# A SwiGLU stream whose tiles take every second half-MiB: from one contiguous block per tile to two interleaved tiles in 16 MiB

## The chip, the cores and the metric

The kernel runs on one NeuronCore of a Trainium2 chip. The metric is device time in microseconds of one execution, as the median of several runs. Beside it there is one profiled execution, whose trace gives every engine instruction and every DMA packet; its "span" runs from the first to the last event that the profile shows on the core.

## The reference

The input `x` is a float32 matrix of 8192 rows by 8192 columns (268.4 MB). Each row is split into a left half `a` and a right half `b` of 4096 columns, and the output is `a * b / (1 + exp(-b))`, a float32 matrix of 8192 by 4096 (134.2 MB):

```python
a, b = np.split(x, 2, axis=-1)
silu_b = b / (1 + np.exp(-b))
return a * silu_b
```

Nothing is reused: every input byte is read once and every output byte is written once, and rows are independent of each other. Which rows are put together in a tile is therefore free.

## The kernel before

A tile holds 256 rows: 128 partitions with `R = 2` consecutive rows each. In DRAM these two rows are 64 KiB of contiguous input, so a tile is a block of 128 x 64 KiB = 8 MiB of input and 128 x 32 KiB = 4 MiB of output. `xv` and `ov` (L30, L31) are the views that say so: row `p` of tile `i` in the view is row `i * 128 + p` of a matrix with 4096 rows of 64 KiB (`xv`) or 32 KiB (`ov`). There are 32 tiles, and three buffers of 64 KiB per partition in SBUF.

`load(i)` (L38 to L44) issues one DMA on SyncE's queue (SP) that brings the whole tile. The last tile is loaded in two halves, one row per partition each. `swiglu(i, k)` (L46 to L54) takes row `k` of each partition: ScalarE (ACT) computes SiLU of the right half in place (L49), and VectorE (DVE) multiplies it with the left half and puts the product where the output is collected, at the front of the same buffer (L50). `store(i)` (L56 to L59) issues one DMA of the 4 MiB product on ACT's queue; the last two tiles use SP's queue instead.

The order of the work is that of the program text, since the schedule is manual (L63). Three loads are issued up front (L67). Then for each tile come two `swiglu` calls, a store, and the load of the tile three further on (L75 to L80), which goes into the buffer that the store has just emptied. That load waits on SP until the store has landed. One small DMA stands ahead of everything: `zt`, 128 partitions of 128 zeros, is written to the front of each output row of tile 0 (L65) and is overwritten later by the first store.

What the change touches is the two views and their three uses, at L43, L58 and L65. The prediction also speaks of the rows that one DMA is made of: a load has 128 pieces of 64 KiB, one per partition, and a store 128 pieces of 32 KiB.

Of the kernel before, what the change touches and what calls it, by code (L numbers as in the profile page):

```python
# [1 line left out]

# [4 lines left out]

_SILU = mybir.ActivationFunctionType.Silu


@with_exitstack
def kernel(
    ctx: ExitStack,
    tc: tile.TileContext,
    x: bass.AP,
    out: bass.AP,
):

    nc = tc.nc
    N, M = x.shape
    half = M // 2
    P = nc.NUM_PARTITIONS
    R = 2
    BUFS = 3

    xv = x.tensor.reshape([N // R, R * M]).ap()  # L30
    ov = out.tensor.reshape([N // R, R * half]).ap()  # L31
    ntiles = N // (P * R)
    last = ntiles - 1

    pool = ctx.enter_context(tc.tile_pool(name="sbuf", bufs=BUFS))
    tiles = {}

    def load(i, rows=None):  # L38
        if i not in tiles:
            tiles[i] = pool.tile([P, R * M], x.dtype, name="xt")  # L40
        lo, hi = (0, R) if rows is None else rows
        nc.sync.dma_start(  # L42
            out=tiles[i][:, lo * M : hi * M], in_=xv[i * P : (i + 1) * P, lo * M : hi * M]  # L43
        )  # L44

    def swiglu(i, k, c0=0, cw=half):  # L46
        xt = tiles[i]
        b = xt[:, k * M + half + c0 : k * M + half + c0 + cw]
        nc.scalar.activation(out=b, in_=b, func=_SILU)  # L49
        nc.vector.tensor_mul(  # L50
            out=xt[:, k * half + c0 : k * half + c0 + cw],
            in0=xt[:, k * M + c0 : k * M + c0 + cw],
            in1=b,
        )  # L54

    def store(i, c0=0, cw=R * half):  # L56
        (nc.scalar if i < last - 1 else nc.sync).dma_start(
            out=ov[i * P : (i + 1) * P, c0 : c0 + cw], in_=tiles[i][:, c0 : c0 + cw]  # L58
        )  # L59


    zt = ctx.enter_context(tc.tile_pool(name="zeros", bufs=1)).tile([P, 128], x.dtype, name="zt")
    ctx.enter_context(tc.manual_schedule())  # L63
    nc.vector.memset(zt, 0.0)  # L64
    nc.scalar.dma_start(out=ov[0:P, 0:128], in_=zt)  # L65

    for i in range(BUFS):  # L67
        load(i)
    for i in range(last):
        for k in range(R):  # L70
            swiglu(i, k)
        if i == last - 1:
            swiglu(last, 0)
        store(i)
        nxt = i + BUFS  # L75
        if nxt < last:
            load(nxt)
        elif nxt == last:
            load(last, (0, 1))
            load(last, (1, 2))  # L80

    store(last, 0, half)
    for c0 in range(0, half, half // 2):
        swiglu(last, 1, c0, half // 2)
    store(last, half, half)


# [1 line left out]
_INS = ['x']  # L89
_OUTS = [((8192, 4096), 'float32')]  # L90


# [23 lines left out]
```

## Time and profile before

| | before |
|---|---|
| median of 3 runs | 936.15 us (936.01 to 936.37) |
| profiled execution, its own time | 935.73 us |
| its span | 933.9 us |
| DVE busy | 283.5 us (30%) |
| ACT busy | 229.4 us (25%) |
| bytes moved by DMA | 402.74 MB, mean 431 GB/s |
| median from issue to landing, 8 MiB load | 34.2 us |
| median from issue to landing, 4 MiB store on ACT's queue | 40.0 us |

The page of the profile gives, per engine, the busy time and its share of the span; for the DMA engines, the busy share in 40 equal slices and the rate in GB/s; for each DMA queue, the packets, the bytes, and the time that its packets took as a share of the time of 16 DMA engines; and the chain of work that ended last. Queue q1 carries SP's transfers (all loads, and the stores of the last two tiles), q10 carries ACT's (all other stores). Times in the views are microseconds from the start of the span.

### The profile page before, as it was taken

The page shows a single profiled execution, that of the slowest core. Times are in us where ns is not written, and L with a number is a line of the kernel's source. Part 1 is how long each engine was busy: PE and PEld are TensorE (multiplying, and loading weights), DVE is VectorE, ACT ScalarE, POOL GpSimd, SP SyncE. Part 2 cuts the span into 40 slices and gives each one's busy share as a digit, 9 for nine tenths or more (in the row PEclk, how much of TensorE's full clock was granted, in tenths as well). Part 3 has the DMA queues.
Part 4 walks back from the last instruction along what each step waited for, and adds up shares of the span by engine and source line. Part 5 has one row for each costly group of instructions (what it writes and reads, how often), then busy time and mean ns, then how long its engine had stood idle before and what let it go on. Part 6 is the DMA issues. An engine that isn't in the chain of part 4 may idle for free.

```text
span 933.9 us, 370 instructions
## 1 busy us (share of the span) xinstructions
DVE 283.5 (30%) x66; ACT 229.4 (25%) x66; POOL 0.2 (0%) x4
## 2 busy tenths in 40 slices
DVE  0333312333113332133321333213332133331252
ACT  0323330233312333113331133311333203332041
POOL 0000000000000000000000000000000000000000
DMA  9999999999999999999999999999999999999998
GB/s 407 422 413 460 411 431 441 449 427 420 456 408 445 431 431 441 435 422 441 448 414 436 435 451 425 429 443 414 446 427 436 436 432 425 439 451 411 441 434 383
DMA packets 9650, 402.74 MB, mean 431 GB/s; under 512 B 1072, under 2 KB 1200, under 8 KB 1200
## 3 DMA queue, kind: packets, MB, share of 16 engines
q1 hardware_dynamic: 5184, 276.83, 68.6%
q10 hardware_dynamic: 4464, 125.90, 31.2%
q14 instruction: 2, 0.02, 0.0%
HBM read 268.44 MB, written 134.28 MB: 431 GB/s over the span
## 4 chain that ended last, share of the span: by engine, by line
DMA 84%; DVE 10%; ACT 4%; DVEq 0%; issue 0%; SPq 0%; ACTq 0%
DMA out_dram<-xt 43%; DMA xt<-in_x_dram 41%; DVE xt L50 10%; ACT xt L49 4%; DVEq L111 0%; SPq L42 0%; ACTq L49 0%; DVEq L50 0%
## 5 line engine op out<-in xcount | busy, mean ns | idle before, releaser
L50 DVE TENSOR_TENSOR xt<-xt 128x4096 f32<-128x4096 f32 (+1 forms) x65 | 283.3, 4360 | 635.8 <-ACT xt L49 632.6
L49 ACT ACTIVATE xt<-xt 128x4096 f32<-128x4096 f32 (+1 forms) x65 | 228.1, 3556 | 686.5 <-DMA xt<-in_x_dram 686.5
L49 ACT ACT_TABLE_LOAD x1 | 1.3, 1283 | 1.5 <-DVE zt L64 1.5
L64 DVE MEMSET zt<- 128x128 f32 x1 | 0.2, 165 | 0.8 <-PEq L100 0.8
L100 POOL MEMSET const-bfloat16-1.0<- 128x1 bf16 x1 | 0.1, 101 | 0.0
L100 POOL MEMSET const-uint8-127<- 128x1 uint8 x1 | 0.1, 101 | 0.0
L100 POOL MEMSET const-float32-0.0<- 128x1 f32 x1 | 0.1, 98 | 0.2 <-issue 0.2
L100 POOL MEMSET const-float32-1.0<- 128x1 f32 x1 | 0.1, 98 | 0.0
## 6 DMA issues: line engine op xcount, KB each, us to landing
out_dram<-xt ACTq DMA_DIRECT2D x30, 4096.0 KB, 40.0
xt<-in_x_dram SPq DMA_DIRECT2D x2, 4096.0 KB, 26.8
out_dram<-xt SPq DMA_DIRECT2D x1, 4096.0 KB, 23.6
out_dram<-xt SPq DMA_DIRECT2D x2, 2048.0 KB, 14.5
xt<-in_x_dram SPq DMA_DIRECT2D x31, 34.2
out_dram<-zt ACTq DMA_DIRECT2D x1, 64.0 KB, 24.1
```

What stands on the lines that cost most here:

```text
L49: nc.scalar.activation(out=b, in_=b, func=_SILU)
L50: nc.vector.tensor_mul(out=xt[:, k * half + c0 : k * half + c0 + cw], in0=xt[:, k * M + c0 : k * M + c0 + cw], in1=b,)
L64: nc.vector.memset(zt, 0.0)
L100: nc = _bacc.Bacc("TRN2", target_bir_lowering=False, num_devices=1)
```

## The change

The two views are laid out anew. Tiles are taken in pairs of 16 MiB of input (8 MiB of output). The pair is cut into `G = 16` groups `e` of 1 MiB (512 KiB of output). In each group the even tile takes the lower half and the odd tile the upper half, and each half holds `P // G = 8` pieces `j` of 64 KiB (32 KiB of output), one for each of 8 neighbouring partitions. Partition `8 * e + j` of tile `i` is thus at `(i // 2) * 16 MiB + e * 1 MiB + (i % 2) * 512 KiB + j * 64 KiB` of the input. The pieces keep their size and are still contiguous; a tile is no longer one block but 16 blocks of 512 KiB, 1 MiB apart.

The DRAM side of every DMA now has three dimensions, 16 x 8 x the piece, where it had two, 128 x the piece. The SBUF side, the order of instructions, the queues, the waits and the arithmetic are the same.

```diff
-    xv = x.tensor.reshape([N // R, R * M]).ap()
-    ov = out.tensor.reshape([N // R, R * half]).ap()
     ntiles = N // (P * R)
+    G = 16
+    xv = x.rearrange("(h e i j r) m -> h i e j (r m)", i=2, e=G, j=P // G, r=R)
+    ov = out.rearrange("(h e i j r) m -> h i e j (r m)", i=2, e=G, j=P // G, r=R)
...
         nc.sync.dma_start(
-            out=tiles[i][:, lo * M : hi * M], in_=xv[i * P : (i + 1) * P, lo * M : hi * M]
+            out=tiles[i][:, lo * M : hi * M], in_=xv[i // 2, i % 2, :, :, lo * M : hi * M]
         )
...
         (nc.scalar if i < last - 1 else nc.sync).dma_start(
-            out=ov[i * P : (i + 1) * P, c0 : c0 + cw], in_=tiles[i][:, c0 : c0 + cw]
+            out=ov[i // 2, i % 2, :, :, c0 : c0 + cw], in_=tiles[i][:, c0 : c0 + cw]
         )
...
-    nc.scalar.dma_start(out=ov[0:P, 0:128], in_=zt)
+    nc.scalar.dma_start(out=ov[0, 0, :, :, 0:128], in_=zt)
```

## The prediction

> **What bounds the kernel now.** I read the page of the profile from the top: engines first, then the DMA slices and the queues.
>
> ```profile
> DVE 283.5 (30%) x66; ACT 229.4 (25%) x66; POOL 0.2 (0%) x4
> ...
> DMA  9999999999999999999999999999999999999998
> ...
> q1 hardware_dynamic: 5184, 276.83, 68.6%
> q10 hardware_dynamic: 4464, 125.90, 31.2%
> ```
>
> No compute engine is busy for a third of the span. The DMA engines are busy in every slice, and the packets of the two queues fill 68.6 + 31.2 = 99.8% of the time of all 16. The row of q1 gives the speed of one DMA engine: 0.686 x 16 x 933.9 = 10,250 engine-us for 276.83 MB, 27.0 GB/s. The row of q10 gives 0.312 x 16 x 933.9 = 4662 engine-us for 125.90 MB, again 27.0 GB/s. Loads and stores go at one and the same speed per engine, so it is not a queue, a direction or the DRAM that holds them up. A 64 KiB piece of a load then costs 2.43 us and a 32 KiB piece of a store 1.21 us. An engine has 8 of each per tile: 8 x 3.64 = 29.1 us, and 32 tiles make 932 us, which with about 2 us of start and end is the span of 933.9.
>
> Next, the chain that ended last and the waits of SP's queue and the engines (line, for what, total us, times, longest):
>
> ```profile
> DMA out_dram<-xt 43%; DMA xt<-in_x_dram 41%; DVE xt L50 10%; ACT xt L49 4%; DVEq L111 0%; SPq L42 0%; ACTq L49 0%; DVEq L50 0%
> ...
> ACT xt L49 <- DMA xt<-in_x_dram: 686.5, 33, 22.8
> DVE xt L50 <- ACT xt L49: 632.6, 33, 25.4
> ...
> SPq L42 <- DMA out_dram<-xt: 868.6, 29, 67.7
> ```
>
> ACT waits some 20 us per tile for a load, SP waits nearly always for a store to land before it can issue the next load. The compute on the chain (14%) doesn't make the DMA idle, since the stage view shows the 16 engines full through the middle (columns: length, DVE, ACT, POOL, clock, DMA share, GB/s):
>
> ```profile
> 200.00:900.00 700.00, 215.71 (x49) 170.93 (x48) 0.00 (x0) 1.00 1.00 434
> ```
>
> So the time is bytes through 16 DMA engines, and nothing can win more than the 0.2% in which they idle, 1.9 us. What can still change is the speed of a piece.
>
> [...]
>
> **The change part by part.** It adds and removes no instruction; every DMA keeps its bytes, its pieces, its queue and its waits. Three things differ.
>
> *Addresses.* Blocks of 512 KiB stand 1 MiB apart. [...] I take 0. Below: at most -1.9 us (the idle share). [...]
>
> *Issue.* A three-dimensional pattern may take longer to issue. An issue on ACT's queue now shows 0.34 us in the timeline. At three times that, ACT loses 0.7 us per tile, out of some 20 us in which it waits for a load; SP's issue comes with 5 us of the previous load still to run (34.2 us to landing against 29.1 per tile). Uncovered it would be 32 x 0.7 = 22 us. What is exposed is the first issue: 0 to +1 us, I take +0.5.
>
> *Which engine serves which partitions.* This decides. [...] The new DRAM side has 16 as its slowest dimension, and one index of it is the 8 neighbouring partitions 8e to 8e + 7. [...]
>
> [...] a load piece 4.86 us, a store piece 2.43 us. With the partners always in the same kind of piece, an engine's cycle of one load and one store piece is 7.28 us where it was 3.64; a tile takes 58.2 us, the kernel 32 x 58.2 + 2 = 1866 us. [...]
>
> [...] For a lead y of one over the other, in us of undisturbed load work and up to 1.21, the cycle is 7.28 - 2y: for 1.21 it is 4.86 us, 1.33 times 3.64[...]. [...] In the packet records of the trace the first pieces of the 16 engines start within 0.73 us, so leads are some tenths of a us. A tile waits for its slowest pair, the one with the least lead among eight: I take y = 0.1, a cycle of 7.08, 1.945 times. Sum: 1.945 x 932 + 2 + 0.5 = 1815 us of span. The profiled execution lay 1.8 us over its span and the median 0.4 over that execution; within the rounding of y, **1815 us**.
>
> The compute doesn't come into it: 12.5 us per tile from landing to product (ACT 3.6, DVE twice 4.4) against a tile period of 58 is less exposed than now.
>
> **The rivals.**
>
> *Partners out of step in kind of piece* (the mechanism above at y near 1.2, or between): 1243 up to 1700. For it: the two queues alternate, and a load piece is twice a store piece, so steps differ easily. Against: the slowest pair rules.
>
> *Partners half a tile apart.* [...] Against: with three buffers a load lands 34.2 us after issue in a period of 29.1, so an engine runs out of loads after a lead of some 5 us, and it needs 14.5. About (14.5 - 5) / 14.5 = 0.65 of the work would still meet: 932 x (1 + 0.65 x 0.33) to 932 x 1.3, that is 1130 to 1210; with deeper queues less, down to 940.
>
> *No loss* (the other side): [...] partitions still dealt out as before. Then the time is 936.2 + 0.5 = 937, not measurably changed. [...]
>
> [...]
>
> *Faster*: bounded by 1.9 us; it would need every idle moment of the DMA engines to vanish.
>
> **How the numbers follow.** Partners [...] in step, 1700 to 1870: 0.50. Out of step, 1210 to 1700: 0.27. Half a tile apart with three buffers' queues, 1130 to 1210: 0.07. Further apart, or addresses alone, 940 to 1130: 0.05. No loss: 0.10. Faster: 0.01. The likeliest gives 1815; its own range is 1700 to 1870. The range 1130 to 1870 leaves out the last three cases, 0.16, and what lies above the full price, some 0.03. A measurement of this kernel can tell about 0.2% (1.9 us) from no change; so slower 0.90, same 0.09, faster 0.01.
>
> **What would show it.** Right: the same packets and bytes per queue, the DMA share still near 100%, but GB/s near half, 216 to 240, in all slices; load and store to landing near or over twice 34 and 40 us; the first three tiles, which have loads alone, at exactly half speed, so that ACT starts about 44 us in where it now starts at 22.8. DVE and ACT busy stay at 283 and 229 us. Wrong: GB/s uneven over the span (a lead that builds up), about 320 [...], or 431 [...]. [...]

## The result

The change makes the kernel slower: 1497.06 us median of 5 (1487.36 to 1529.26) against 936.01 before (935.76 to 936.37). The ratio is 1.594, with a 95% interval of 1.590 to 1.599. A ratio, here and below, is taken only from the executions within 1.5% of the fastest of their kernel, here three of the five, so this one belongs to about 1492 us. The profiled execution took 1512.57 us with a span of 1510.8, one of the longer ones of the five.

The page of the changed kernel answers row by row to the one before: engines, DMA slices with their rates, queues (packets, MB, share of the time of 16 engines), and transfers with the time to landing.

```profile
DVE 283.5 (19%) x66; ACT 229.4 (15%) x66; POOL 0.2 (0%) x4
...
DMA  9999999999999999999999999999999999999997
GB/s 210 233 263 276 283 281 286 277 282 300 272 283 285 278 267 277 273 266 266 251 276 272 262 257 263 273 256 273 257 264 280 257 256 270 262 265 269 271 256 216
...
q1 hardware_dynamic: 5184, 276.83, 77.4%
q10 hardware_dynamic: 4464, 125.90, 21.9%
...
out_dram<-xt ACTq DMA_DIRECT2D x30, 4096.0 KB, 57.9
...
xt<-in_x_dram SPq DMA_DIRECT2D x31, 70.4
```

The rate row of before, slice by slice, was this:

```profile
GB/s 407 422 413 460 411 431 441 449 427 420 456 408 445 431 431 441 435 422 441 448 414 436 435 451 425 429 443 414 446 427 436 436 432 425 439 451 411 441 434 383
```

The busy times of DVE and ACT, and the packets and bytes of the two queues, are those of before to the last digit, and the DMA engines are again busy all the time. Only the rate has gone down. The two queue rows say by how much for each kind of piece. q1: 0.774 x 16 x 1510.8 = 18,710 engine-us for 276.83 MB, 14.8 GB/s, or 4.43 us for a 64 KiB piece of a load, where it was 2.43. q10: 0.219 x 16 x 1510.8 = 5294 engine-us for 125.90 MB, 23.8 GB/s, or 1.38 us for a 32 KiB piece of a store, where it was 1.21. In time of one engine the row of q1 grows by 529 us (0.774 x 1510.8 less 0.686 x 933.9) and that of q10 by 40: 568 of the 577 us between the spans. So nearly all of the loss is on the queue of the loads. The rest is time in which DMA engines idle, most of it at the end. The rate row shows where the loss is: 210 in the first slice, in which there are loads alone, half of the 407 of before; between 250 and 300 from the third slice to the last but one.

The timeline shows the same at the start (start, length, instruction, idle before), first before and then after:

```profile
22.77 7.12 ACT L49 ACTIVATE xt<-xt 128x4096 f32<-128x4096 f32 x2 [20.03 <-DMA xt<-in_x_dram]
```

```profile
44.27 7.12 ACT L52 ACTIVATE xt<-xt 128x4096 f32<-128x4096 f32 x2 [41.31 <-DMA xt<-in_x_dram]
```

Tile 0 is complete after 44.27 us where it was after 22.77. The waits are as many as before and longer (line, for what, total us, times, longest):

```profile
ACT xt L52 <- DMA xt<-in_x_dram: 1259.1, 33, 41.3
...
SPq L45 <- DMA out_dram<-xt: 1401.7, 29, 109.6
```

The chain that ended last is of no use here: it gives 94% to "another core or an unknown queue", so it doesn't find what released most of its steps.

### The profile page after: what moved, and what is told of

Its sections match the earlier page's. It is cut to its first block, busy times and chain, and to the rows that moved or that the text cites. A ratio compares the mean times of both kernels' runs of the same rounds, so it can differ in the third digit from the quotient of the medians.

```text
span 1510.8 us, 370 instructions
## 1 busy us (share of the span) xinstructions
DVE 283.5 (19%) x66; ACT 229.4 (15%) x66; POOL 0.2 (0%) x4
## 3 DMA queue, kind: packets, MB, share of 16 engines
q1 hardware_dynamic: 5184, 276.83, 77.4%
q10 hardware_dynamic: 4464, 125.90, 21.9%
## 4 chain that ended last, share of the span: by engine, by line
another core or an unknown queue 94%; DMA 3%; SPq 1%; ACT 0%; DVE 0%; DVEq 0%; issue 0%; ACTq 0%
DMA xt<-in_x_dram 3%; SPq L45 1%; ACT xt L52 0%; DVE xt L53 0%; DVEq L114 0%; ACTq L52 0%
## 6 DMA issues: line engine op xcount, KB each, us to landing
out_dram<-xt ACTq DMA_DIRECT2D x30, 4096.0 KB, 57.9
xt<-in_x_dram SPq DMA_DIRECT2D x31, 70.4
```

## Experiments

The theory is that of the prediction: with 16 groups of 8 neighbouring partitions the DMA engines share in pairs, the two of a pair having together the 27.0 GB/s that one had before. Two engines that share are called partners here, and the expectations call this the port theory. That they share in pairs was the author's estimate. What the runs show of it is the rates of the ladder below (197 GB/s with 16 groups and 408 with 32, and 54 for four engines as for two); where two engines meet, and which two, no run shows. Its rivals are the addresses (blocks 1 MiB apart in DRAM) and the three-dimensional pattern as such. The packet records named below are the trace's list of all DMA packets with start, length and size; they don't name the engine.

**Keep the interleaving, restore the split.** One number is changed: 32 groups of 4 partitions.

```diff
-    G = 16
+    G = 32
```

> The change with 32 groups of 4 partitions in place of 16 groups of 8: tiles are still interleaved in pairs within 16 MiB, each DMA is still a three-dimensional pattern, but the slowest dimension has 32 entries[...]. Port theory [...]: the loss vanishes, 936 to 938 us, ACT starts at about 22.8 us. Address theory (blocks that stand apart in DRAM are slow): still clearly slower, 1300 to 1500 us. Issue theory (three-dimensional patterns are slow to generate): still 1500.

Measured: 937.12 us (936.28 to 937.67), ratio 1.0009 (1.0003 to 1.0016). Its queue rows:

```profile
q1 hardware_dynamic: 5184, 276.83, 68.5%
q10 hardware_dynamic: 4464, 125.90, 31.2%
```

The tiles are as interleaved as in the change, with blocks of 256 KiB in 512 KiB, and every DMA has three dimensions, yet the loss is gone: only the slowest dimension is 32 and not 16. The pattern as such is thereby ruled out as the cause, and so is interleaving by itself. What remains is 0.9 us. The timeline has an issue on ACT's queue at 0.55 us (0.34 before) and tile 0 at 23.25 us (22.77 before), so about half of it is seen at the start.

**Keep the split, restore the addresses.** A tile is one contiguous block again; the sixteen groups take its pieces in turn.

```diff
-    xv = x.rearrange("(h e i j r) m -> h i e j (r m)", i=2, e=G, j=P // G, r=R)
-    ov = out.rearrange("(h e i j r) m -> h i e j (r m)", i=2, e=G, j=P // G, r=R)
+    xv = x.rearrange("(i j e r) m -> i e j (r m)", e=G, j=P // G, r=R)
+    ov = out.rearrange("(i j e r) m -> i e j (r m)", e=G, j=P // G, r=R)
...
-            out=tiles[i][:, lo * M : hi * M], in_=xv[i // 2, i % 2, :, :, lo * M : hi * M]
+            out=tiles[i][:, lo * M : hi * M], in_=xv[i, :, :, lo * M : hi * M]
...
-            out=ov[i // 2, i % 2, :, :, c0 : c0 + cw], in_=tiles[i][:, c0 : c0 + cw]
+            out=ov[i, :, :, c0 : c0 + cw], in_=tiles[i][:, c0 : c0 + cw]
...
-    nc.scalar.dma_start(out=ov[0, 0, :, :, 0:128], in_=zt)
+    nc.scalar.dma_start(out=ov[0, :, :, 0:128], in_=zt)
```

> Each tile is one contiguous block of 8 MiB again, as before the change, but the pieces are dealt out the other way round: partition 8e + j takes piece 16j + e of the block, so that the DMA pattern is 16 x 8 pieces with 16 slowest. Port theory: as slow as the change, 1450 to 1550 us, ACT starts at about 44 us. Address theory: 936 to 940 us, since at any time the 16 engines read from one contiguous megabyte.

Measured: 1494.71 us median of 4 (1450.34 to 1551.65); the ratio is 1.552 (1.549 to 1.555), which belongs to about 1453 us. Tile 0 is there at the same time as in the change:

```profile
44.04 7.12 ACT L50 ACTIVATE xt<-xt 128x4096 f32<-128x4096 f32 x2 [41.09 <-DMA xt<-in_x_dram]
```

Without the interleaving the kernel is about as slow as with it, so the addresses are not the cause of the loss. That they have a small share is not excluded: by the ratios this kernel loses 517 us where the change loses 556, but the executions of the two overlap.

**Only the loads.** The loads keep 16 groups of 8, the stores go back to 128 pieces.

```diff
-    ov = out.rearrange("(h e i j r) m -> h i e j (r m)", i=2, e=G, j=P // G, r=R)
+    ov = out.tensor.reshape([N // R, R * half]).ap()
...
-            out=ov[i // 2, i % 2, :, :, c0 : c0 + cw], in_=tiles[i][:, c0 : c0 + cw]
+            out=ov[i * P : (i + 1) * P, c0 : c0 + cw], in_=tiles[i][:, c0 : c0 + cw]
...
-    nc.scalar.dma_start(out=ov[0, 0, :, :, 0:128], in_=zt)
+    nc.scalar.dma_start(out=ov[0:P, 0:128], in_=zt)
```

> Loads as in the change (16 groups of 8), stores as before (128 pieces, contiguous block). The products go to other rows than the reference's, since loads and stores name different rows; bytes, pieces, instructions and waits are those of the change. Port theory [...]: stores at 1.21 us a piece, loads at 4.86 while the partner loads: 1243 us [...] to 32 x 8 x 6.07 = 1555 us; ACT starts at 44 us. Port theory with one rate for both directions: at or above the 1497 us of the change less what stores lose there, 1400 to 1700.

Measured: 1536.25 us median of 4 (1519.19 to 1548.17), ratio 1.627 (1.622 to 1.631).

```profile
q1 hardware_dynamic: 5184, 276.83, 77.6%
q10 hardware_dynamic: 4464, 125.90, 22.0%
```

With its span of 1517.4 us, q1 gives 4.46 us a load piece and q10 1.39 us a store piece. The stores go in 128 pieces without groups here, as before the change, and are just as slow as in it (1.39 and 1.38 us), so the split costs the stores of the change nothing that can be seen; what is common to both kernels is the slow loads beside the stores. Undoing the stores' half of the change gains nothing.

**Only the stores.** The other half: `xv` and the load as before the change, `ov` and the stores as in it.

> Loads as before (128 pieces, contiguous block), stores as in the change (16 groups of 8). The products go to other rows than the reference's; bytes, pieces, instructions and waits are the same. Port theory with separate directions: loads stay at 2.43 us, a store piece is between 1.21 and 2.43: 936 us (partners never store together) to 32 x 8 x 4.86 = 1245 us (always); in the change's profile a store piece took about 1.4, which would give 32 x 8 x 3.8 = 980 us. ACT starts at 22.8 us. One rate for both directions: loads are slowed by the partner's stores too, above 1100 us.

Measured: 990.89 us (983.92 to 1011.08), ratio 1.056 (1.052 to 1.061).

```profile
q1 hardware_dynamic: 5184, 276.83, 68.0%
q10 hardware_dynamic: 4464, 125.90, 31.3%
```

The span is 986.4 us: 2.54 us a load piece (2.43 before), 1.29 a store piece (1.21). If partners had one rate for loads and stores together, or if two partners that store always took twice their time, this kernel would by the estimates recorded ahead be above 1100 us. At 990.89 us neither is the case. In the packet records 88% of the store pieces take the 1.21 us of the kernel before.

That is not because partners store at different times. In the packet records of this kernel's first store the engines go in step: its pieces come in rounds of 16, one per engine, and in each round from the third of eight on, 15 of the 16 pieces start within 0.6 us and the other one about as long before them. So in these rounds, however the engines are paired, both of a pair store at once in at least seven of the eight pairs. All 128 pieces of that store take 1.21 us all the same, and the load that runs beside it lands 29.0 us after the one before it, as in the kernel before. The loss of 55 us comes after that; the landings of one load, at first 0.6 to 3 us apart between the engines, are then up to 12 us apart.

**The sharing by itself.** A ladder with no compute and no overlap: one 8 MiB load after another, split with another slowest dimension each time, then 4 MiB stores in the same way. It was executed once.

```python
def view(t, rows, G):
    v = t[0:rows, :]
    if G == P:
        return v.rearrange("(p r) m -> p (r m)", r=R)
    return v.rearrange("(j e r) m -> e j (r m)", e=G, j=P // G, r=R)
...
for G in (128, 64, 32, 16, 8, 4, 2):
    nc.sync.dma_start(out=xt, in_=view(x, P * R, G))
for G in (128, 64, 32, 16, 8, 4, 2):
    nc.sync.dma_start(out=view(out, P * R, G), in_=xt[:, 0 : R * half])
```

> The disputed cost by itself: no compute and no overlap. One load of the same contiguous 8 MiB block after another, each waiting for the one before, its pieces dealt out with 128, 64, 32, 16, 8, 4 and 2 as the slowest dimension; then the same seven ways for one store of 4 MiB each. Nothing else is computed, so the output is not the reference's. An engine alone moves 27 GB/s. Port theory: loads of 128, 64, 32: 19.4 us each plus about 2; 16: 38.8; 8: [...] 77.6; 4: [...] 155; 2: [...] again 155. If only the number of engines counts: 19.4, 19.4, 19.4, 19.4, 38.8, 77.6, 155. Stores half of each. [...]

Stages of the ladder, cut inside the loads of 32, 16, 8, 4 and 2 in that order (columns: stretch, its length, POOL, clock, busy share of 16 DMA engines, GB/s):

```profile
50.00:63.00 13.00, 0.00 (x0) 1.00 0.94 408
75.00:107.00 32.00, 0.00 (x0) 1.00 0.95 197
120.00:190.00 70.00, 0.00 (x0) 1.00 0.50 105
200.00:345.00 145.00, 0.00 (x0) 1.00 0.25 54
360.00:505.00 145.00, 0.00 (x0) 1.00 0.13 54
```

The busy share tells the engines at work: 16, 16, 8, 4, 2. The last two rows decide: four engines, a quarter of the sixteen, move 54 GB/s, and two engines, an eighth, also move 54. So the four have the rate of two, as they would in two pairs, and the two the 27 GB/s each of the kernel before. Likewise eight engines move 105, the rate of four, and sixteen move 408 with 32 groups and 197 with 16. From the packet records, in us from first to last piece:

```text
slowest dimension   128    64    32    16     8     4     2
load  8 MiB        20.4  20.6  20.9  41.0  80.3 156.8 155.6
store 4 MiB         9.9   9.9   9.9  20.0  38.1  68.0  77.8
```

The loads follow the port theory in every column, within 3 us. Stores alone do so too, but for four engines, where 68.0 is below 77.8. So with nothing else going on, stores too go at half the rate with 16 groups: 20.0 us where it was 9.9.

The stores of the change don't pay for that: in its packet records 2 of the 3840 store pieces on ACT's queue take over 2 us. Partners that keep out of each other's way would explain it, but the records speak against that. In the change's first store the 16 engines start their first pieces within 1.37 us of each other and all 16 are in flight together at one moment, yet none takes over 1.47 us. If partners shared one engine's rate while both store, pieces that start so close together would have to be longer: by an estimate from these starts and 1.21 us for a piece by itself, some would take 1.8 us or more, however one pairs them. Nor do the 336 store pieces that have on average eight or more others in flight take longer (1.35 us) than the 383 with fewer than two (1.41).

**How stores and slow loads add up.** The changed kernel without its stores, but for one row per partition of the last tile:

```diff
             swiglu(last, 0)
-        store(i)
...
-    store(last, half, half)
```

> The change with the stores left out, but for one row per partition of the last tile; most of the output is not written. Loads and compute as in the change. Loads alone, [...] 256 pieces of 4.86 us, 1244 us and some 10 for start and end, at 216 GB/s.

And with half of each store:

```diff
             swiglu(last, 0)
-        store(i)
+        store(i, 0, half)
...
-    store(last, half, half)
```

> The change with half of every store left out: one row of the two per partition, pieces of 16 KiB; half of the output is not written. Theory A, a load gains while its partner stores [...]: the same as without stores, 1244 to 1260 us, and the 1497 of the whole change would come from something that begins with larger stores. Theory B, a load gains next to nothing while its partner stores, so stores are added to loads at about their own length: 256 x (4.86 + 0.61) = 1400 us less a few per cent, 1350 to 1400, halfway between no stores and the change.

Measured: 1300.81 us without stores (1298.27 to 1302.82, ratio 1.389 with 1.387 to 1.391), 1379.35 with half of them (1352.05 to 1390.02, ratio 1.453 with 1.442 to 1.464, which belongs to about 1361 us). The queue rows, without stores first:

```profile
q1 hardware_dynamic: 4896, 270.53, 99.7%
```

```profile
q1 hardware_dynamic: 5040, 272.63, 85.8%
q10 hardware_dynamic: 4464, 62.98, 14.0%
```

Without stores a load piece takes 0.997 x 16 x 1297.9 us for 270.53 MB, 5.02 us: 26.1 GB/s for two engines together, 3% under the 27.0 of one engine. That makes the kernel some 50 us longer than expected. By the ratios half stores add some 60 us and full ones 191, where 256 pieces at their own length would add 155 and 310. Neither theory holds as it stood. With half stores the time lies in the interval of theory B, but only because the loads alone take 47 us more than it assumed. A load piece is shorter when there are stores, 4.46 us beside half stores and 4.43 beside whole ones, but by less than theory A needs: there the stores would add nothing and 1301 us would be the time of the whole change. And it is about as much shorter beside stores of half the length. So some two fifths of the half stores' own length are added, and three fifths of the whole ones'.

The records of the landings (one per engine and transfer: 1072 for the 67 transfers of the change) show one thing that goes with it. Without stores the 16 engines finish a load within 1.1 us of each other, from the first to the last tile. In the change this grows from 1.1 us in the first load to 32 us in the twelfth and is about 20 in the second half; for its stores it reaches 43 us, nearly a whole tile. With half stores it grows to 11.5 us for loads; before the change it was at most 1.9 for loads and 3.0 for stores. Which engine has which partner is not in the records, so whether partners drift from each other or pairs from other pairs is open.

The drift brings no gain. The rate of the change falls meanwhile, and with only the loads split it stays the same although the loads' spread grows from 6 us to 30 (two stretches of the change, then two of that kernel; columns: stretch, length, DVE, ACT, POOL, clock, DMA share, GB/s):

```profile
200.00:500.00 300.00, 53.11 (x12) 42.74 (x12) 0.00 (x0) 1.00 1.00 283
800.00:1100.00 300.00, 53.10 (x12) 42.73 (x12) 0.00 (x0) 1.00 1.00 265
```

```profile
200.00:900.00 700.00, 127.58 (x29) 106.83 (x30) 0.00 (x0) 1.00 1.00 266
900.00:1400.00 500.00, 93.66 (x22) 71.22 (x20) 0.00 (x0) 1.00 1.00 266
```

Two things stay open: why stores with 16 groups go at half the rate when they run alone (20.0 us for 9.9) and not beside loads (1.21 us a piece in the first store), and what shortens the loads when there are stores, and by so little. It is not that partners must be out of step for it: in the change the 16 load pieces that follow the first round of stores start within 1.24 us of each other and take 3.98 to 4.65 us. For the stores the numbers above give an estimate that fits both cases but is tested by no run: two store pieces one after the other take 2 x 1.21 = 2.43 us, and a cycle of one load and one store piece is 3.62 us long in the first stores of the kernel with only the stores split, so it has room for both. In the ladder store follows store, and there is no such room.

## Why the prediction was right in its cause and too high in its size

*What bounds the kernel.* Right. The DMA engines were full before and after, and 568 of the 577 us between the spans are in the length of pieces. Compute is untouched.

*Addresses, 0 us.* Right in the main: contiguous tiles with the same split are about as slow (1494.71 us), interleaved ones with 32 groups are not slow (937.12).

*Issue, +0.5 us.* Right in size: with 32 groups 0.9 us in all.

*Which engine serves which partitions.* Right in its effect: with the slowest dimension alone changed, the ladder's loads go at 197 GB/s for 16 and at 408 for 32, and four engines move 54 as two do. How the partitions are dealt out to the engines was the author's estimate, and it is not shown: the busy share tells how many engines work, not which partitions they serve.

*The load piece beside a partner's load, 4.86 us.* Twice the 2.43 us of before, an estimate. Right for loads alone, and a little low: 5.02 without stores, tile 0 at 44.27 us as forecast.

*The store piece beside a partner's store, 2.43 us.* This is the step that failed. The prediction took partners to be in step in kind all along, with a lead of y = 0.1, and a cycle of 7.08 us; that a lead shortens the cycle by 2y was its estimate. Measured are 4.43 + 1.38 = 5.81. A cycle of 7.08 with that lead splits into about 4.75 for the load and 2.33 for the store, so of the 1.27 us too much 0.95 are the store's and 0.32 the load's; times 256 they are 325 us, close to the 304 between 1815 and the profiled span. The price does exist when stores run alone (20.0 us where it was 9.9). Beside loads it isn't paid: with only the stores changed the kernel took 991 us, not the 1245 of partners in step. And it isn't paid even where the partners are in step: the 128 pieces of that kernel's first store take 1.21 us each. So what failed is not the size of the lead but the price that the lead was to lower. Nor does one lead hold all along for the engines as a whole: they part once loads and stores are mixed (up to 32 us between the landings of one load), and with loads alone they don't (1.1 us). Why they part is not known.

*The rivals.* "Partners out of step in kind of piece", given 0.27 with 1210 to 1700, has the measured time in its interval; the likeliest case, 1700 to 1870 with 0.50, was missed. That the time fell inside the whole range is thus in part luck, since this rival's mechanism is not what the records show: the stores are short with partners in step too. Nor does its sum fit, for by 7.28 - 2y a store piece of 1.38 us (y = 1.05) goes with a cycle of 5.18, and 5.81 were measured. Its lower end of 1243, where loads use every pause of the partner, wasn't reached: the loads alone take 1301. "Half a tile apart" isn't what ruled: partners so far apart would by that rival load in 2.43 us a piece, and in the change's packet records 14 of 3968 take under 2.7. The largest rival on the other side, no loss, falls with the ladder.

*What would show it.* ACT started 44.27 us in, as said. "Near half, in all slices" held at the two ends of the rate row alone; "load and store to landing near or over twice" held for the load (70.4 against 34.2), not for the store (57.9 against 40.0). Both misses are for the most part the missing store price. Of the signs of being wrong, a rate that is uneven over the span is there in part: 283 GB/s from 200 to 500 us and 265 from 800 us on.

## What to carry to other kernels

Look at the slowest dimension of a DMA's DRAM view, not only at the size of its pieces: in the ladder the same 128 pieces of 64 KiB ran at 408 or at 197 GB/s, with 32 or 16 there. If a DRAM view has to be blocked, block it so that its slowest dimension has 32 or 64 entries for 128 partitions (4 or 2 partitions to a block); in the ladder these loads took 20.9 and 20.6 us, against 20.4 with 128. When two kinds of transfer share the engines, don't add their worst prices: a price that is real when a transfer runs alone (20.0 us for 9.9 in the ladder's stores) may not be paid when the engines alternate (1.21 us a piece in the first store with only the stores split), even with all of them doing the same at the same time. So measure each kind alone and both together. And when a cost is missing, look whether the meeting that should cause it took place: in that first store 15 of 16 pieces started within 0.6 us in each round from the third on, and it cost nothing.

## What the runs showed of the hardware that was not expected

- With 16 groups two engines together don't quite reach one engine's rate: 5.02 us a load piece against twice 2.43, about 3% worse over a whole kernel of loads.
- A store piece takes 2.5 us in the middle of the ladder's store with 16, and 1.21 us in the first store of the kernel with only the stores split, where every engine alternates between loads and stores.
- Engines that only load, with 16 groups, stay within 1.1 us of each other for 32 tiles; once stores are mixed in, as in the change, they finish the same load up to 32 us apart and the same store up to 43, and the executions of one and the same kernel then spread by some per cent (1450 to 1552 us for the contiguous tiles with 16 groups), where those of the kernel before agree within 0.2%.
- Stores in 128 pieces without groups take 1.39 us a piece in place of 1.21 when the loads beside them are slow (4.46 us a piece in place of 2.43).
- With stores alone, four engines finished in 68.0 us, less than the 77.8 of two; the loads show no such gain (156.8 and 155.6).
